# A diffusion transformer layer on one core: forward retention states made beside the last projection chunk, and retention and output tiles paced at 36 attention slots

## The chip, the core and the metric

The kernel runs on one core of a Trainium2 chip. The metric is the device time of one execution in microseconds. The core has a matmul engine (TensorE, PE in the profile; PEld is its weight load), a vector engine (VectorE, DVE), a scalar engine (ScalarE, ACT), GpSimd (POOL) and SyncE (SP), which issues the transfers here. Each engine works through its own queue of instructions in order and waits on semaphores for the others.

## The reference

One layer takes 2048 latent rows and 256 context rows of width 1024. All arithmetic is float32.

```python
h  = rmsnorm(x, norm1_g) * (1 + sc1) + sh1           # sh, sc, g: c_act @ w_mod + b_mod
hc = rmsnorm(ctx, norm1_g) * (1 + csc1) + csh1
rq, rk, rv, rg, aq, ak, av = split(h @ w_in)         # 512 512 512 512 512 128 128
crk, crv, cak, cav = (the same columns of) hc @ w_in # the context needs no others
# retention, 4 heads of 128, chunks of 128 rows, both directions, started from the context's state
o_fwd[c] = (q_c k_c^T * decay) v_c + q_c S_c * q_dec
S_(c+1)  = S_c * c_dec + (k_c * k_dec)^T v_c
ret = groupnorm(o_fwd + flip(o_bwd)) * gn_g * silu(rg)
# attention, 8 query heads on 2 key heads of 64, keys: 256 context + 2048 latent rows
att = softmax(rmsnorm(q) rope . rmsnorm(k) rope / 8) v
x = x + g1 * (concat(ret, att) @ w_out)              # w_out 1024 x 1024
x = x + g2 * (relu(h2 @ w_ff1) ** 2 @ w_ff2)         # h2 = rmsnorm, modulate; width 4096
out = rmsnorm(x, final_norm_g)
```

## The kernel before, in words

The float32 products are made of float16 ones. A factor is split into a high and a low part (`hi`, `lo`), and three matmuls (high by high, low by high, high by low) add up in one PSUM bank. In the traces they stand as three neighbouring lines: 638 to 640 in the projection, 1420 to 1422 in the output, 1668 to 1670 in the up product and 1728 to 1730 in the down product. Turns (transposes) and the retention products stay float32, as 128x128 matmuls.

**Start and projection.** Rows come in 18 tiles of 128: 0 and 1 are context, 2 to 17 latent (`x_c`, `x_l`). Ahead of the plan, code written out in order makes the modulation (`mods`, four quarters of `w_mod`) and prepares the first tiles: `squares` (line 444, ACT), `root` (lines 80 and 81, POOL), `normal` (line 450, DVE), then for each half p of the columns `turn_h` (line 459, PE), `modulate` (line 464 on DVE, 465 on POOL), `high_h` (line 469, ACT) and `low_h` (line 473, DVE). `first.fetch`, `bound`, `split` load the first weight chunk (`w_in` in four pairs of blocks), take its absolute bounds (line 506) and split it (lines 535, 536). `halves_h(p, ms)` does the four steps of a half for several tiles. Then comes the plan: `at(q, step, fn)` puts a step at clock q, and a loop over q runs the steps in the order `dma, mm, turn, copy, work, mix, extra, store`. A row of the projection (one tile by one column chunk, 24 matmuls) takes two clocks. The column chunks go in the order RV, RK, AKV, AQ, RG, RQ, of 18, 18, 18, 16, 16 and 16 rows; `base[col]` is a chunk's first clock. The row's bank is evacuated by ACT (line 645, `xs`).

Beside the rows the plan has other work: rope on DVE and POOL (lines 671, 674, 686) and the turn of its result (line 691), the norms of AKV and AQ heads (`ys`, `kn`; lines 723, 736), the turn of keys (`turn_key`, line 741), maxima over rows of weights (`maxima`; turns at line 386, `macc` at line 381), the tables of decay (`decay_tables`, ACT exponentials and a logarithm, lines 947 to 975), and the first maxima of the attention. The last are products of queries and keys, 18 pieces for each of the first groups (lines 167 and 171, PE), each followed by a DVE maximum (line 180, `nm`). Before the attention starts, `least` (lines 186 to 198) turns these into an extra row of the query.

**Attention.** 32 groups (a query tile by a key head) of 18 key pieces each, one piece to a slot k. `on(k, phase, fn)` puts an event at slot k, and the phases of a slot run in the order of `PHASES`. Scores start at slot 22 and take two matmuls a slot (lines 204 and 205); ACT makes the exponential (line 210) and its float16 part (line 214), DVE and POOL the rest (lines 221, 223), and PE the product with the values (lines 237, 238). Events in the same slots do the retention: `retention(24)` first makes 17 forward and 2 backward states, two slots each (a load of `rk` and `rv`; `weigh`, line 1229, POOL; `product`, line 1235, four matmuls; `update`, line 1245, DVE; a store of the forward state). From `R0 = 66` on, every `RF = 35` slots, a tile is made from the last to the first: three products (lines 1268 to 1270), and 43 slots later its output tile (`output_tile`: turn at line 1405, output product at lines 1420 to 1422). The first FF half needs the output tiles as well: the row norm (lines 1434, 1441, 1154, 1155), the normal `xr` (line 1447, POOL) that takes the new x back from memory, its turn (line 1452) and modulation (lines 1457, 1462). `output_weights(44)` loads and scales `w_out` (lines 1372, 1377).

**FF.** `prelude(done)` puts the first steps of the feed-forward part at the slots behind the last score (`done` = 606): loads and sums of `w_ff1` (`sum_w1`, line 1597, POOL), products (`up_part`), `gate_first` (line 1626, POOL). The loop runs to the slot of the last output tile's end; behind it FF runs to the end by itself.

## Time and profile before

| what | us |
|---|---|
| runs | 2898.58, 2898.51, 2896.85; median 2898.51 |
| profiled execution, its own time | 2894.32 |
| its span | 2892.2 |
| PE busy in the span | 2728.7 (94%) |
| stage: to the first latent turn | 0 to 62.6 |
| projection chunks, RV to the last evacuation | to 624 |
| attention, first score to last score | 632 to 1577.5 |
| from there to the first down matmul | to 1633.2 |
| FF to the end | to 2892 |

The profile's numbers belong to one execution, whose own time is 2894.32, so its span of 2892.2 covers nearly all of it. A row of the timeline gives start and duration; the bracket behind it is how long the engine had been idle and what released it. Matmuls of 128x512 issue every 0.216 us one behind the other, and their shown durations overlap. A row of the windows gives the window, its length, the busy time of the engines with the count of their instructions, the granted clock of PE, the share of DMA and the GB/s.

### The profile page before, as it was taken

How to read it: one execution, taken by the hardware profiler on the slowest of the kernel's cores; microseconds unless marked ns; L12 is line 12 of the kernel's file. 1: busy time of each engine (PE TensorE's matmuls, PEld its weight loads, DVE VectorE, ACT ScalarE, POOL GpSimd, SP SyncE). 2: the span in 40 equal slices, each digit the busy share in tenths (PEclk: the TensorE clock that was granted, in tenths of full speed). 3: DMA queues.
4: the chain of work that ended last, by engine and by line, in shares of the span. 5: the costliest groups of instructions: out<-in, count | busy, mean ns of one | idle time of the engine just before them, and what ended most of it. 6: DMA issues, size and time to landing. Idle time of an engine off the chain costs nothing. (4 is left out here: it accounts for less than half of the span.)

```text
span 2892.2 us, 45242 instructions
## 1 busy us (share of the span) xinstructions
PE 2728.7 (94%) x17152; PEld 1459.3 (50%) x17152; DVE 2094.2 (72%) x3324; ACT 1428.9 (49%) x2418; POOL 1528.8 (53%) x1289
## 2 busy tenths in 40 slices
PE   5999999988899998899999899999999999999998
PEld 2545644446566665566666344444444444444443
DVE  4556687667878777787785577777777777777776
ACT  3533762336777777777777333333333333333332
POOL 2523782338757568885667566664443434444432
PEclk8999999999999999999999999999999999999999
DMA  6478758337212213332113722231114411111111
GB/s 220 153 232 290 237 157 259 108 105 241 60 48 66 84 58 101 119 116 67 50 61 124 266 81 77 82 116 58 59 49 152 164 59 59 55 51 47 52 44 59
DMA packets 251320, 324.26 MB, mean 112 GB/s; under 512 B 106775, under 2 KB 157975, under 8 KB 249310
## 3 DMA queue, kind: packets, MB, share of 16 engines
q1 hardware_dynamic: 251102, 321.37, 34.5%
q8 instruction: 135, 2.21, 0.3%
q14 instruction: 83, 0.68, 0.1%
HBM read 249.84 MB, written 71.46 MB: 111 GB/s over the span
## 5 line engine op out<-in xcount | busy, mean ns | idle before, releaser
L180 DVE TENSOR_REDUCE nm<-mp 128x1 f32<-128x512 f32 (+1 forms) x576 | 389.5, 683 | 153.4 <-PE mp L167 124.6
L221 POOL TENSOR_TENSOR plo<-p,phi 128x1024 f16<-128x1024 f32 x160 | 353.1, 2208 | 165.6 <-ACT phi L214 136.2
L210 ACT ACTIVATE p<-st 128x512 f32<-128x512 f32 x576 | 337.8, 597 | 175.6 <-PE st L205 113.0
L1728 PE MATMUL pd<-w2hi,uhi 128*128 128x512 f16 x1024 | 388.1, 379 | 13.6 <-DVE acc L1731 13.3
L1729 PE MATMUL pd<-w2lo,uhi 128*128 128x512 f16 x1024 | 388.1, 379 | 0.6 <-DVE w2lo L72 0.6
L1730 PE MATMUL pd<-w2hi,ulo 128*128 128x512 f16 x1024 | 388.1, 379 | 0.0
L1731 DVE SCALAR_TENSOR_TENSOR acc<-pd,sc,acc 128x512 f32<-128x512 f32 x512 | 366.0, 738 | 5.7 <-PE pd L1730 5.6
L1668 PE MATMUL pu<-hf,w1f 128*128 128x512 f16 x896 | 340.3, 380 | 2.9 <-DVE q L1691 2.2
L1669 PE MATMUL pu<-hf,w1f 128*128 128x512 f16 x896 | 340.4, 380 | 0.0
L1670 PE MATMUL pu<-hf,w1f 128*128 128x512 f16 x896 | 340.2, 380 | 0.0
L214 ACT ACTIVATE phi<-p 128x1024 f16<-128x1024 f32 x288 | 303.9, 1055 | 0.0
L638 PE MATMUL pso<-whi,h 128*128 128x512 f16 (+1 forms) x816 | 294.9, 361 | 0.4 <-ACT whi L535 0.4
L639 PE MATMUL pso<-wlo,h 128*128 128x512 f16 (+1 forms) x816 | 294.5, 361 | 0.2 <-DVE wlo L536 0.2
L640 PE MATMUL pso<-whi,h 128*128 128x512 f16 (+1 forms) x816 | 294.5, 361 | 0.0
L237 PE MATMUL o<-wv,plo 128*128 128x65 f16 x2304 | 235.4, 193 | 22.9 <-POOL plo L221 16.8
L223 DVE TENSOR_TENSOR plo<-p,phi 128x512 f16<-128x512 f32 x256 | 236.1, 923 | 18.9 <-ACT phi L214 16.2
L238 PE MATMUL o<-wv,phi 128*128 128x129 f16 x2304 | 243.2, 221 | 0.0
L237 PEld LDWEIGHTS <-plo 128*128 128x128 f16 x2304 | 206.7, 98 | 57.3 <-POOL plo L221 25.6
L204 PE MATMUL st<-qr,ks 128*128 128x512 f16 x576 | 220.5, 383 | 15.1 <-ACT p L210 14.9
L1680 POOL TENSOR_TENSOR r<-r 128x512 f32<-128x512 f32 x64 | 66.3, 1039 | 295.2 <-ACT r L1679 295.2
L205 PE MATMUL st<-qr,ks 128*128 128x512 f16 x576 | 220.7, 383 | 1.1 <-DVE qr L198 1.0
L238 PEld LDWEIGHTS <-phi 128*128 128x128 f16 x2304 | 205.8, 98 | 20.0 <-issue 0.3
(326 smaller groups left out, 5393.9 us busy)
## 6 DMA issues: line engine op xcount, KB each, us to landing
wm<-in_w_ff SPq DMA_DIRECT2D x64, 512.0 KB, 5.2
w1r<-in_w_ff SPq DMA_DIRECT2D x64, 512.0 KB, 4.3
ws<-in_w_ff SPq DMA_DIRECT2D x124, 256.0 KB, 3.3
wmr<-in_w_mod SPq DMA_DIRECT2D x32, 512.0 KB, 5.5
hf<-hp SPq DMA_DIRECT2D x56, 256.0 KB, 3.2
hf<-hf SPq DMA_DIRECT2D x14, 1024.0 KB, 6.1
wst<-in_w_in SPq DMA_DIRECT2D x20, 512.0 KB, 6.1
orv<-rv SPq DMA_DIRECT2D x35, 256.0 KB, 3.0
```

What stands on the lines that cost most here:

```text
L180: nc.vector.tensor_reduce(dst, src, axis=AX.X, op=ALU.max, negate=True)
L210: nc.scalar.activation(self.p[kt // 2][:, kt % 2], self.s.pop(kt), AF.Exp, scale=HD**-0.5)
L221: nc.gpsimd.tensor_tensor(lo, p, hi, op=ALU.subtract)
L237: mm(o[:, : HD + 1], lo[:, i, c], v[:, : HD + 1], start=False, stop=False)
L238: mm(o, hi[:, i, c], v[:, :VW], start=False, stop=last)
L1668: mm(pu[i], whi, hi, start=k == 0, stop=False)
L1669: mm(pu[i], whi, lo, start=False, stop=False)
L1670: mm(pu[i], wlo, hi, start=False, stop=k == 3)
L1728: mm(ps, uh, wh, start=f == 0, stop=False)
L1729: mm(ps, uh, wl, start=False, stop=False)
L1730: mm(ps, ul, wh, start=False, stop=f == NF - 1)
L1731: nc.vector.scalar_tensor_tensor(acc[:, c], ps, sc2, acc[:, c], op0=ALU.mult, op1=ALU.add)
```

## The change

It has three parts. At the start the loads change places (all of the first weights ahead of x tiles 2 and 3), tile 2 goes from the written order into the plan, and the steps of tiles 0 and 1 stand among the splits in another order. In the plan, ten of the rows of maxima go into RV; the decay tables go from RQ to AKV and are cut in parts; the turns of keys and of queries come a clock later, and AQ goes from its last row to its first; the parts of the values go to RG; the first maxima of groups 0 and 1 are made in RG and those of group 2 in RQ; and the 17 forward states are made in RQ (15 of them, and two at the end) from the stores of RK and RV, every 29/16 clocks. In the attention only two backward states are left ahead of the tiles; tiles start at slot 34 every 36 slots; `output_weights` starts at slot 26; and the loop runs to the last event of all. The last output tile starts at slot 617 instead of 634.

```diff
@@ -278,7 +278,8 @@
             base[col] = 2 * len(slots)
-            slots += [(n, m) for m, t in enumerate(TILES) if t[0] == "l" or col not in (C_RQ, C_RG, C_AQ)]
+            ms = [m for m, t in enumerate(TILES) if t[0] == "l" or col not in (C_RQ, C_RG, C_AQ)]
+            slots += [(n, m) for m in (ms[::-1] if col == C_AQ else ms)]
@@ -472,10 +473,11 @@
-        for m in range(3, len(TILES)):
-            q = 2 * (m - 3)
+        for m in range(2, len(TILES)):
+            q = 2 * (m - 2)
...
                 at(max(0, q - 6), "dma", load_x, m)
+            if m > 2:
@@ -610,9 +612,9 @@
                     at(q + 2, "work", self.head_norm, 8)
-                    at(q + 3, "turn", self.turn)
-                    at(q + 4, "copy", self.split_turned)
-                    at(q + 5, "store", self.store_turned, aq_d)
+                    at(q + 4, "turn", self.turn)
+                    at(q + 5, "copy", self.split_turned)
+                    at(q + 6, "store", self.store_turned, aq_d)
@@ -625,8 +627,8 @@
                     at(q + 5, "copy", self.high_key)
-                    at(q + 6, "turn", self.turn_key)
-                    at(q + 7, "work", self.keep_key)
+                    at(q + 7, "turn", self.turn_key)
+                    at(q + 8, "work", self.keep_key)
@@ -939,28 +941,31 @@
-            def rates():
+            def rates(part):
...
...
             at(q0, "dma", load)
-            at(q0 + 3, "extra", rates)
-            for h in range(4):
-                at(q0 + 5 + h, "extra", tables, h)
-            at(q0 + 9, "extra", rest)
+            for i in range(4):
+                at(q0 + 6 + 2 * i, "extra", rates, i)
+                at(q0 + 14 + 3 * i, "extra", tables, i)
+            at(q0 + 26, "extra", rest)
+        def forward_states(c, q):
+            x = {}
+            def load():
+                x["k"] = sg.tile([P, 2, 512], F32, name="rkv", tag="wm")
+                for i, src in enumerate((rk_d, rv_d)):
+                    nc.sync.dma_start(x["k"][:, i], src[c])
+            def weigh():
+                x["w"] = sg.tile([P, 4, P], F32, name="rkw", tag="wmr")
+                k = x["k"][:, 0].rearrange("p (h d) -> p h d", h=4)
+                nc.gpsimd.tensor_tensor(x["w"], k, bc(kd[:, 0].unsqueeze(2), [P, 4, P]), op=ALU.mult)
+            def product():
+                x["ps"] = psM.tile([P, 4, P], F32, name="mpr", tag="mps", bufs=1)
+                for h in range(4):
+                    v = x["k"][:, 1, h * P : (h + 1) * P]
+                    mm(x["ps"][:, h], x["w"][:, h], v, start=True, stop=True)
+            def update():
+                old = states.get("s")
+                s = states["s"] = sg.tile([P, 4, P], F32, name="rst", tag="wst", bufs=4)
+                if old is None:
+                    nc.scalar.activation(s, x["ps"], AF.Copy)
+                    return
+                for h in range(4):
+                    nc.vector.scalar_tensor_tensor(
+                        s[:, h], old[:, h], cd[:, 0, h : h + 1], x["ps"][:, h], op0=ALU.mult, op1=ALU.add
+                    )
+            def store():
+                nc.sync.dma_start(sf_d[c - 1].rearrange("p (h d) -> p h d", h=4), states["s"])
+            at(q - 5, "dma", load)
+            at(q - 2, "mix", weigh)
+            at(q, "turn", product)
+            at(q + 1, "work", update)
+            if c > 0:
+                at(q + 1, "store", store)
...
             at(q_load, "dma", g.minima, kp)
+            assert len(qs) == NK
...
         rk, akv, aq, rg, rq = (base[c] for c in (C_RK, C_AKV, C_AQ, C_RG, C_RQ))
-        row_slots = [rk + 2 * i + 1 for i in range(18)] + [rg + 2 * i + 1 for i in range(14)]
+        row_slots = [11 + 2 * i for i in range(10)] + [rk + 2 * i + 1 for i in range(18)]
+        row_slots += [rg + 2 * i + 1 for i in range(4)]
@@ -1006,12 +1054,15 @@
             maxima(n, q)
-        value_parts(aq + 4)
-        decay_tables(rq)
-        ff_scales(rq + 13)
-        first_maxima(0, xp, "x", 4, rg + 8, [rg + 13 + i for i in range(18)])
-        first_maxima(1, sg, "wst", 4, rq, [rq + 4 + i * 12 // 17 for i in range(18)])
-        first_maxima(2, sg, "wst", 4, rq + 10, [rq + 17 + i * 12 // 17 for i in range(18)])
+        decay_tables(akv)
+        value_parts(rg + 2)
+        ff_scales(rq + 5)
+        states, end = {}, base["end"]
+        for c in range(NK - 1):
+            forward_states(c, rq + 4 + c * 29 // 16)
+        first_maxima(0, hp, "h0", 1, aq + 20, [rg + i * 16 // 18 for i in range(NK)])
+        first_maxima(1, hp, "h1", 1, aq + 24, [rg + 16 + i * 16 // 18 for i in range(NK)])
+        first_maxima(2, hp, "h0", 1, rg + 20, [rq + 2 + 2 * i for i in range(14)] + [end, end, end + 1, end + 1])
@@ -1027,8 +1078,8 @@
         loads = [[lambda q=q, k=k: mods[q].load(k) for k in range(0, KT, 2)] for q in range(4)]
-        between = [[lambda: load_x(0), lambda: load_x(1)], [lambda: load_x(2), lambda: first.fetch(0)]]
-        between += [[lambda k=k: first.fetch(k) for k in (2, 4, 6)], [lambda: load_x(3)]]
+        between = [[lambda: load_x(0), lambda: load_x(1)], [lambda k=k: first.fetch(k) for k in (0, 2)]]
+        between += [[lambda k=k: first.fetch(k) for k in (4, 6)], [lambda: load_x(2), lambda: load_x(3)]]
@@ -1047,12 +1098,9 @@
-        def halves_h(p, ms):
-            for m in ms:
-                turn_h(m, p)
-                modulate(m, p)
-                high_h(m, p)
-                low_h(m, p)
+        def first_half(m):
+            for fn in (turn_h, modulate, high_h, low_h):
+                fn(m, 0)
@@ -1060,26 +1108,28 @@
         mods[1].shift_and_scale()
-        modulation(2, (ready, 2), (halves_h, 0, (0,)), (first.bound, 0), (halves_h, 0, (1,)))
+        modulation(2, (first_half, 0), (first.bound, 0), (first_half, 1), (first.bound, 2))
...
         mods[2].shift_and_scale()
-        modulation(3, (halves_h, 0, (2,)), (first.bound, 2), (first.bound, 4), (first.bound, 6))
+        modulation(3, (first.bound, 4), (first.bound, 6))
...
         first.greatest()
+        modulate(0, 1)
         first.spread()
-        modulate(0, 1)
+        turn_h(1, 1)
         first.scales()
+        first.split(0)
...
         low_h(0, 1)
-        first.split(0)
         first.split(2)
-        halves_h(1, (1,))
+        modulate(1, 1)
         first.split(4)
+        high_h(1, 1)
+        low_h(1, 1)
         first.split(6)
-        halves_h(1, (2,))
-        ready(3)
+        ready(2)
@@ -1094,10 +1144,10 @@
+    pp = pool(attn, "pp", 3)
+    op = pool(attn, "op2", 2)
     qp = pool(attn, "qp")
-    op = pool(attn, "op2", 2)
     vp = pool(attn, "vp")
-    pp = pool(attn, "pp", 3)
@@ -1199,14 +1249,14 @@
     rp = pool(room, "rp", side="right")
-    BUFS = {"orv": 3, "ork": 2, "okw": 2, "oo": 2, "sf": 2, "sb": 2, "ma": 2}
+    BUFS = {"orv": 3, "ork": 2, "okw": 2, "oo": 2, "sb": 2, "ma": 2}
...
-    RF, R0 = 35, 66
+    RF, R0 = 36, 34
@@ -1246,9 +1296,6 @@
-        def keep_state(i):
-            nc.sync.dma_start(sf_d[i], x["s", i].rearrange("p h d -> p (h d)"))
@@ -1301,23 +1348,15 @@
-        SF = 2
-        todo = [(0, c) for c in range(NK - 1)] + [(1, 1), (1, 0)]
-        for n, (d, c) in enumerate(todo):
-            k = k0 + SF * n
+        for n, c in enumerate((1, 0)):
+            k = k0 + 2 * n
             on(k - 5, "dma", take, c, "rk", "rv")
-            on(k - 2, "late", weigh, d, c)
-            on(k, "pe", product, c, n % 2, (0, 1))
-            on(k + 1, "pe", product, c, n % 2, (2, 3))
-            if d == 0:
-                old, to, tag = None if c == 0 else ("s", c - 2), ("s", c - 1), "sf"
-            else:
-                old, to, tag = None if c == 1 else ("b", NT), ("b", NT - 1 + c), "sb"
-            on(k + 1, "late", update, d, c, old, to, tag, (0, 1))
-            on(k + 2, "late", update, d, c, old, to, tag, (2, 3))
-            if d == 0 and c > 0:
-                on(k + 3, "dma", keep_state, c - 1)
-        assert k0 + SF * len(todo) + 2 <= R0
+            on(k - 2, "late", weigh, 1, c)
+            on(k, "pe", product, c, n, (0, 1))
+            on(k + 1, "pe", product, c, n, (2, 3))
+            old = None if c == 1 else ("b", NT)
+            on(k + 1, "late", update, 1, c, old, ("b", NT - 1 + c), "sb", (0, 1))
+            on(k + 2, "late", update, 1, c, old, ("b", NT - 1 + c), "sb", (2, 3))
@@ -1489,7 +1528,7 @@
         for q in range(2):
-            at = k + (31 if t == 1 else 27) + q
+            at = k + (32 if t == 1 else 27) + q
@@ -1537,8 +1576,8 @@
     done = attention()
-    retention(24)
-    output_weights(44)
+    retention(25)
+    output_weights(26)
@@ -1786,7 +1825,7 @@
     with tc.manual_schedule():
-        for k in range(min(events)[0], max(made_at + 1, last) + 1):
+        for k in range(min(events)[0], max(events)[0] + 1):
```

Line numbers behind the first edit shift by 1 or 2, and those behind `decay_tables` by 39 to 50: 1420 to 1422 become 1459 to 1461, 1447 becomes 1486, 1597 becomes 1636, 1668 to 1670 become 1707 to 1709, and 1728 becomes 1767. The steps of a forward state are lines 1001 (load), 1006 (weigh), 1012 (product), 1018 and 1021 (update) and 1026 (store).

On ACT, at the start, ahead of the first square of a tile that the plan's first turn needs, there stood (`h` is the high half of a modulated tile, `ws` the bounds and `whi` the split of the first weights):

```order
L469 ACTIVATE h_535<-t 128x512
L506 ACTIVATE junk,ws<-wst 128x512 x6
L469 ACTIVATE h_479<-t 128x512
L535 ACTIVATE whi<-wst,ws 128x512 x4
L469 ACTIVATE h_502<-t 128x512
L535 ACTIVATE whi<-wst,ws 128x512 x4
L469 ACTIVATE h_535<-t 128x512
```

and now there stands:

```order
L470 ACTIVATE h_490<-t 128x512
L508 ACTIVATE junk,ws<-wst 128x512 x6
L537 ACTIVATE whi<-wst,ws 128x512 x2
L470 ACTIVATE h_467<-t 128x512
L537 ACTIVATE whi<-wst,ws 128x512 x4
L470 ACTIVATE h_490<-t 128x512
L537 ACTIVATE whi<-wst,ws 128x512 x2
L445 ACTIVATE junk,ss<-x_l_371 128x1024
```

The third tile's halves are gone from this place, and the splits stand in pairs between the halves of the first two.

On DVE, at the end of RQ, the last rows of the projection (`t` and `ys` are the rope, `unit` and `mt` open the attention) read before:

```order
L671 TENSOR_TENSOR t_6481<-xs,tb_6388 128x512
L180 TENSOR_REDUCE nm<-mp 128x2
L686 TENSOR_TENSOR ys<-t_6481,t_6482 128x512
L671 TENSOR_TENSOR t_6511<-xs,tb_6439 128x512
L686 TENSOR_TENSOR ys<-t_6511,t_6512 128x512
L1112 TENSOR_TENSOR unit<-ident 128x1
```

and now, with `rst` for the forward states:

```order
L673 TENSOR_TENSOR t_6753<-xs,tb_6661 128x512
L1021 SCALAR_TENSOR_TENSOR rst<-rst,cd,mpr 128x128 x4
L688 TENSOR_TENSOR ys<-t_6753,t_6754 128x512
L180 TENSOR_REDUCE nm<-mp 128x1 x2
L1021 SCALAR_TENSOR_TENSOR rst<-rst,cd,mpr 128x128 x4
L180 TENSOR_REDUCE nm<-mp 128x1
L180 TENSOR_REDUCE nm<-mp 128x2
L1162 TENSOR_TENSOR unit<-ident 128x1
```

Two states' updates and four maxima stand behind the last row's first rope step.

On POOL, in the tail behind the last score, the normal of the last output tile (`xr`) stood behind the sums of the up weights (`w1s`) and the gated down weights (`w2r`):

```order
L1597 TENSOR_TENSOR w1s<-w1r 128x512
L1462 TENSOR_TENSOR u<-u,s_240 128x512 x2
L1597 TENSOR_TENSOR w1s<-w1s,w1r 128x512
L1626 TENSOR_TENSOR w2r<-w2r,g2h 128x512 x2
L1597 TENSOR_TENSOR w1s<-w1r 128x512
L1626 TENSOR_TENSOR w2r<-w2r,g2h 128x512
L1680 TENSOR_TENSOR r<-r 128x512
L1626 TENSOR_TENSOR w2r<-w2r,g2h 128x512
L1597 TENSOR_TENSOR w1s<-w1r,w1s 128x512
L1154 TENSOR_SCALAR cv_f<-ss 128x1
L1155 TENSOR_TENSOR cy_f<-cv_f,half 128x1
L1447 TENSOR_SCALAR xr<-xr,cy_f 128x1024
```

and now stands ahead of them:

```order
L1204 TENSOR_SCALAR cv_f<-ss 128x1
L1205 TENSOR_TENSOR cy_f<-cv_f,half 128x1
L1486 TENSOR_SCALAR xr<-xr,cy_f 128x1024
L1636 TENSOR_TENSOR w1s<-w1r 128x512
L1636 TENSOR_TENSOR w1s<-w1s,w1r 128x512
L1665 TENSOR_TENSOR w2r<-w2r,g2h 128x512 x2
L1636 TENSOR_TENSOR w1s<-w1r 128x512
```

`xr` of the last tile has moved up past four of the sums and four of the gated weights.

37 lines of the change are left out of this document (20 added, 17 removed).

## The prediction

> **What bounds the kernel now.** I read the page's busy shares first, then the windows of the stages, then the waits, chain and timeline inside the stages that the diff touches. TensorE bounds the whole.
>
> ```profile
> PE 2728.7 (94%) x17152; PEld 1459.3 (50%) x17152; DVE 2094.2 (72%) x3324; ACT 1428.9 (49%) x2418; POOL 1528.8 (53%) x1289
> ```
>
> 94% is a mean over stages, so the stages are laid side by side. The rows are the first 48.7 us, the projection chunks AKV, AQ and RQ, the tail behind the last score, and FF.
>
> ```profile
> 0.00:48.70 48.70, 27.57 (x162) 10.55 (x163) 16.95 (x70) 13.64 (x30) 8.19 (x18) 0.87 0.85 285
> 276.40:334.20 57.80, 52.92 (x473) 46.06 (x472) 31.24 (x105) 45.04 (x108) 33.08 (x78) 1.00 0.79 247
> 334.20:427.10 92.90, 90.41 (x452) 45.20 (x450) 72.34 (x123) 59.08 (x112) 75.97 (x84) 1.00 0.60 185
> 523.50:625.00 101.50, 98.27 (x485) 48.38 (x483) 66.19 (x157) 28.14 (x52) 30.45 (x36) 1.00 0.27 83
> 1578.00:1633.00 55.00, 47.35 (x265) 23.80 (x264) 25.88 (x43) 19.87 (x39) 31.09 (x32) 0.97 0.84 317
> 1633.00:2892.00 1259.00, 1229.78 (x5682) 555.56 (x5680) 932.77 (x1213) 426.00 (x686) 567.24 (x432) 1.00 0.24 78
> ```
>
> The first two numbers are length and busy PE. The projection is nearly full (RQ 98.3 of 101.5), so an instruction put into PE's order there costs its issue time. FF, the last row, is the same code in the same order: 0. What can be won is idle PE at the start, waits inside the chunks, slots of attention that are long for another engine's sake, and the tail.
>
> **A, the start.** This is the longest gap of PE in the kernel.
>
> ```profile
> 53.29 0.63 ACT L469 ACTIVATE h<-t 128x512 f16<-128x512 f32 x1 [2.75 <-POOL t L465]
> 59.12 0.63 ACT L469 ACTIVATE h<-t 128x512 f16<-128x512 f32 x1 [2.75 <-POOL t L465]
> 62.63 1.09 PE L459 MATMUL psx<-ident,x_l 128*128 128x128 f32 x4 [10.51 <-DVE x_l L450]
> DMA  0598899999999999999997250385000000002898
> ```
>
> ACT waits twice for POOL (2.75 each), once for the half of tile 1 and once for that of tile 2, ahead of the square (line 444) that releases the next tile. In the new order tile 1's modulation stands on DVE ahead of split 4, so that the first wait has splits under it, and tile 2 has left this chain (second wait, and its 0.63). That is 2.75 + 2.75 + 0.63 = 6.1: **−6**. All of it lies on the path, since PE waits for the end of this chain alone. x tiles 2 and 3 are now issued on SP's queue behind all pairs of w_in halves, but the same transfers stand ahead of the last of them. The last row above is the DMA share over 0 to 75 us, 1.9 us a digit: these loads are over by 53, so a later tile 2 is still in time for a square at 54 or so. Bounds: 0, where it lands late by as much as ACT gains, and −10.5, the whole gap; I take the value that the two waits show.
>
> **B, the projection.** The change adds 15 forward states (a POOL product, four fp32 matmuls, four DVE updates, a load and a store each) to RQ. Ten rows of maxima (a turn on PE and DVE work each) go from RG to RV, pieces of the first maxima from RQ to RG, the decay tables from RQ to AKV. Prices on PE:
>
> ```profile
> 663.94 0.61 PE L1235 MATMUL bank<-orv,okw 128*128 128x128 f32 x4
> 664.38 0.38 PE L204 MATMUL st<-qr,ks 128*128 128x512 f16 x1
> 1592.76 0.38 PE L1421 MATMUL bank<-wo,ah 128*128 128x512 f16 x1
> 1592.98 0.38 PE L1422 MATMUL bank<-wo,al 128*128 128x512 f16 x1
> ```
>
> Four fp32 products issue in 0.44 (663.94 to 664.38), one 128x512 matmul in 0.22 (start to start; the shown 0.38 overlaps). The waits, and the pieces in RQ:
>
> ```profile
> PE psx L741 <- DVE kn L736: 4.5, 5, 1.4
> PE psx L691 <- DVE ys L723: 4.0, 4, 1.7
> PE mps L386 <- DVE macc L381: 1.7, 2, 0.9
> PE mp L167 <- DVE nm L180: 1.8, 4, 1.0
> L180 DVE TENSOR_REDUCE nm<-mp 128x1 f32<-128x512 f32 (+1 forms) x36 | 23.8, 683 | 0.5 <-PE mp L167 0.4
> ```
>
> - RV: ten rows of a 0.44 turn would be 4.4; PE's idle behind the start gap takes most of it, and I take +1.4 (bounds 0 and 4.4).
> - AKV: turn_key one step later removes most of 4.5 (−4.3); the decay tables move onto ACT there.
>
> ```profile
> 528.90 0.69 ACT L645 ACTIVATE xs<-pso,wm 128x512 f32<-128x512 f32 x1 [4.43 <-PE pso L640]
> 529.61 1.28 ACT L947 ACT_TABLE_LOAD   x1
> 530.90 0.21 ACT L947 ACTIVATE dw<-dw 128x8 f32<-128x8 f32 x1
> 531.13 1.28 ACT L949 ACT_TABLE_LOAD   x1
> 537.72 1.28 ACT L972 ACT_TABLE_LOAD   x1
> ```
>
>  Three loads (3.9) and 4.7 of small exponentials are 8.6 us more on ACT, which is busy 45.0 of 57.8 there. The cover is its 12.8 of idle time, but the tables fall on the chunk's first two thirds, and ACT's evacuations free PE's banks behind them: I take +3.0 as not covered (bounds 0 and 8.6). Sum −1.3. Silu and Exp each need one reload more, two times 1.28, of which the first stands ahead of an evacuation in RG that has slack of 4.4 (the first row above) and the second ahead of the first attention exponential.
> - AQ: turn one step later, −4.0, the whole row of waits.
> - RG: 36 pieces where 18 were, 18 × 0.22 = +3.9, less the 1.7 of waits for macc, as ten rows have left: +2.2.
> - RQ: of the 36 pieces (x36) 14 stay. 15 × 0.44 = +6.6, 22 × 0.22 = −4.8, waits for nm −1.0, and +2 for products that find rk and rv not landed: +2.8. Their loads (17 of 512 KB) stand in SP's queue among the stores, in a window with a DMA share of 0.27, so they should rarely be late; who waits behind a late product is the row of projection matmuls on PE, hence ACT's evacuation. Bounds 0 and 15 (1 us a product). POOL and DVE cover the rest: 15 products of 1.2 (below) on a POOL busy 30.5 of 101.5, 60 updates of 0.34 against 22 maxima of 0.68 less, on a DVE busy 66.
> - Handover: DVE has eight updates (0.34 each, in C) and four maxima (0.68) more behind the last evacuation:
>
> ```profile
> 624.07 0.69 ACT L645 ACTIVATE xs<-pso,wm 128x512 f32<-128x512 f32 x1 [2.27 <-PE pso L640]
> 633.68 0.58 PE L205 MATMUL st<-qr,ks 128*128 128x512 f16 x1 [0.99 <-DVE qr L198]
> ```
>
>  From evacuation to first score product 633.68 − 624.07 = 9.6 now, with PE waiting for DVE. Of the 5.4 us of DVE that come in, I let its waits for ACT and POOL there take 3.1: +2.3 (bounds 0 and +5.4).
>
> Sum of B: 1.4 − 1.3 − 4.0 + 2.2 + 2.8 + 2.3 = **+3.4**.
>
> A rule weighed against these rows: the Trainium skill, "ScalarE: Activation LUTs", section "What ACT_TABLE_LOAD costs", puts a switch at about 1.28 us of load plus 1.38 us of drain. By it the three loads in AKV would take 8.0, not 3.9, and the sum would come out some 4 us higher. The trace agrees on the load and not on the drain: 528.90 + 0.69 is 529.59, the load starts at 529.61 and the exponential at 530.90.
>
> **C, attention, slots 22 to 597.** Line 204 issues once a slot, so windows cut at its count give slot lengths: 12 slots (46 to 57), 180, 120 and 168.
>
> ```profile
> 666.80:694.00 27.20, 5.01 (x13) 1.29 (x13) 0.87 0.94 306
> 773.30:1065.60 292.30, 68.16 (x180) 17.54 (x181) 1.00 0.20 63
> 1065.60:1269.80 204.20, 45.90 (x121) 11.71 (x120) 0.98 0.34 99
> 1269.80:1545.00 275.20, 63.64 (x169) 16.36 (x168) 1.00 0.23 72
> ```
>
> Slots 46 to 57 take 27.2, where 12 at the later 1.62 take 19.5; the DMA share is 0.94 there. Between 658 and 694:
>
> ```profile
> ACT wo L1377 <- POOL wos L1372: 8.7, 2, 7.1
> PE bank L1235 <- POOL okw L1229: 5.3, 5, 3.2
> L1245 DVE SCALAR_TENSOR_TENSOR sf<-sf,cd,bank 128x128 f32<-128x128 f32 x36 | 10.5, 341 | 15.7 <-DMA sf<-sf 12.9 <-PE bank L1235 2.8
> L1229 POOL TENSOR_TENSOR okw<-ork,kd 128x512 f32<-128x512 f32 x10 | 11.7, 1170 | 5.0 <-DMA ork<-rk 5.0
> ```
>
> All but the wait for wos belong to forward states, which leave; output weights come earlier, onto emptier slots. So 27.2 goes to about 19.2: **−8**, the last retention states and the first tile (slot 34) taking the place of the rest at the rate of a later slot. On PE the stage is even: 17 states out (17 × 0.44 = 7.5), the last output tile in. Bounds: −15.5, where those 7.5 are time as well, and +10, if the output tile's work (10 us of PE, in D) lands on slots with no room.
>
> **D, the tail.** From the last score to the first down matmul:
>
> ```profile
> 1577.46 0.38 PE L205 MATMUL st<-qr,ks 128*128 128x512 f16 x1
> 1604.39 0.66 PE L1452 MATMUL bank<-ident,xr 128*128 128x128 f32 x4 [1.77 <-POOL xr L1447]
> 1627.25 1.12 POOL L1447 TENSOR_SCALAR xr<-xr,cy_f 128x1024 f32<-128x1024 f32 x1 [5.11 <-DMA x<-xr]
> 1628.42 0.66 PE L1452 MATMUL bank<-ident,xr 128*128 128x128 f32 x4 [3.89 <-POOL xr L1447]
> 1633.19 0.38 PE L1728 MATMUL pd<-w2hi,uhi 128*128 128x512 f16 x1
> ```
>
> 1633.19 − 1577.46 = 55.7. The last output tile now starts at slot 617 rather than 634. Behind the last score the program's order has 60 output matmuls instead of 96: 36 × 0.22 = 7.8, with 2 of products and turns that go along, about 10. Of the waits 3.89 goes and 1.4 of the 1.77, because the last tile's normal (xr) comes before the up matmuls run out: 5.3. That makes −15.3. What is late next: POOL's xr waits for a store of x to land (5.11), and in the new order it stands ahead of w1 sums for the up matmuls, so these queue behind the wait, and PE behind them. I give back 4 of the 5.1: **−11** (bounds −18, with the second wait gone and nothing given back, and 0).
>
> Sum: −6 + 3.4 − 8 − 11 = −21.6 against the profiled execution's 2894.3, so 2872.7. The median of the runs, 2898.5, stands 4.2 above; the forecast in its terms is **2877**.
>
> **Rivals.**
> - More than that (0.15): no late product, no give-back on POOL: −6 + 0 − 10 − 15 = −31, so 2867. For it: POOL is busy only 31 of 55 in the tail, and RQ's DMA is at 0.27. Against it: xr has waited for x in the last tiles already, whoever was behind it.
> - The tail's gain is lost (0.18): D = 0, since the first down matmul waits for POOL's w2 products behind the store, whenever PE is done with the tile; 2888. For it: the 5.11, and a DMA share of 0.84 in that window. Against it: the up matmuls, 28 rows of work, stand between.
> - No measurable change (0.14): the 15 products wait for rk and rv on PE, at 1.1 us each +16.5 in place of +2 (the row for sf has 12.9 in 6, 2.2 a time): −21.6 + 14.5 = −7, and with a start held by its loads −1: 2892 to 2898.
> - Slower (0.08), by one mechanism: at 36 slots per tile every tile begins at the same phase of the 18-slot group (at 35 the phase moves by one a tile). If that phase is the crowded one, all 576 slots run like slots 286 to 405: 204.2/120 = 1.70 against 292.3/180 = 1.62 and 275.2/168 = 1.64. 576 × 0.06 = +35 or so: 2877 + 35 = 2912. It decides from 1.69 a slot on (27 us). Against it: 16 tiles passed through 16 phases before, and both long windows are level.
>
> **How the numbers follow.** The forecast has 0.45, with its own range 2868 to 2889. All four parts at their better end give −10.5 + 0 − 15.5 − 15 = −41, 2858, the low end; the high end is the no-change case's, 2898, above which the slower case (0.08) lies. 0.2% is 5.8 us, about what can be told from no change. Faster: 0.45 + 0.15 + 0.18, and 0.01 of the no-change case, which begins just below 2892.7: 0.79; the same 0.13; slower 0.08.
>
> **What would show it.** PE's first gap ends near 56 instead of 62.6 (A). AKV and AQ lose their waits for kn and ys; RQ's length stays within 2 us of 101.5, with no PE wait for rkv (B). Slots 46 to 57 take about 19 (C). Last score to first down takes about 45, and POOL has xr before w1s (D). The prediction is wrong if the slot rate passes 1.68, if RQ grows by over 10 us, or if the tail keeps 55.

## The result: slower by 1.4%, and the profile after

| | before | changed |
|---|---|---|
| runs, median | 2897.68 (2892.78 to 2898.58) | 2938.52 (2936.88 to 2939.62) |
| span of the profiled execution | 2892.2 | 2937.8 |

The ratio is 1.0144, with a 95% interval of 1.0130 to 1.0158. Forecast were 2877 and a range of 2858 to 2898, so the forecast missed in sign. Each of the three things that the prediction named as showing it wrong came true: a slot rate over 1.68 (1.702 over slots 124 to 555), RQ over 10 us longer (11.0), and a tail that keeps its 55 (54.7).

The lengths of the stages, from the start of a stage's first matmul to that of the next, come from the two traces:

| stage | before | changed | difference | the prediction's term |
|---|---|---|---|---|
| to the first projection matmul | 48.8 | 45.2 | −3.6 | A: −6, with the first gap, which lies in RV |
| RV | 123.3 | 126.5 | +3.2 | +1.4 |
| RK | 104.4 | 104.9 | +0.5 | 0 |
| AKV | 57.7 | 64.0 | +6.3 | −1.3 |
| AQ | 93.0 | 89.6 | −3.4 | −4.0 |
| RG | 96.4 | 100.5 | +4.1 | +2.2 |
| RQ, to its last matmul | 99.8 | 110.8 | +11.0 | +2.8 |
| handover to the first score | 8.7 | 9.6 | +0.9 | +2.3 |
| first to last score | 945.2 | 961.7 | +16.5 | C: −8 |
| last score to first down matmul | 55.9 | 54.7 | −1.2 | D: −11 |
| FF from there | 1259.0 | 1270.1 | +11.1 | 0 |

The windows of the changed kernel that answer to those of before are these: the time to the first matmul, AKV, AQ, RQ, the tail and FF.

```profile
0.00:45.20 45.20, 25.80 (x154) 8.39 (x155) 14.27 (x66) 11.34 (x26) 6.42 (x15) 0.92 0.93 307
276.60:340.60 64.00, 55.66 (x473) 47.11 (x472) 38.20 (x138) 51.53 (x127) 33.57 (x80) 0.97 0.72 228
340.60:430.30 89.70, 89.70 (x449) 44.99 (x447) 66.33 (x111) 58.40 (x109) 72.19 (x87) 1.00 0.61 184
530.80:641.60 110.80, 107.48 (x576) 59.83 (x574) 64.45 (x157) 19.64 (x31) 47.87 (x48) 0.98 0.52 172
1613.00:1667.70 54.70, 39.92 (x216) 19.62 (x215) 18.96 (x25) 15.03 (x28) 28.27 (x26) 0.89 0.82 317
1667.70:2937.00 1269.30, 1234.77 (x5680) 556.59 (x5679) 944.96 (x1223) 429.36 (x692) 570.53 (x435) 0.99 0.24 76
```

AQ is full (89.7 busy of 89.7): there the change did what it says. RQ is full too, and longer: it carries more PE work than the prediction counted. AKV is longer with PE idle for 8.3 of 64. The tail has PE idle for 15 of 54.7. FF has the code of before, and its 10.3 us more than in the row of before are 5.3 of idle PE and 5.0 of busy PE (1234.77 against 1229.78, for as many matmuls). The granted clock of the row is 0.99 instead of 1.00.

The start, in the timeline, with the first gap and the two places in RV where PE waits for DVE:

```profile
55.40 1.12 PE L460 MATMUL psx<-ident,x_l 128*128 128x128 f32 x4 [4.52 <-DVE x_l L451]
...
114.43 0.63 PE L460 MATMUL psx<-ident,x_l 128*128 128x128 f32 x4 [1.82 <-DVE x_l L451]
115.78 1.46 PE L387 MATMUL mps<-macc,ones 128*32 128x512 f32 x2 [0.73 <-DVE macc L382]
```

The first gap fell from 10.51 to 4.52, by the 6.0 that were forecast; RV gave it back, in part here.

A forward state in RQ, in PE's timeline, and the count of its products over the whole run:

```profile
561.53 1.05 PE L1012 MATMUL mpr<-rkv,rkw 128*128 128x128 f32 x8
562.42 0.38 PE L640 MATMUL pso<-whi,h 128*128 128x512 f16 x1
...
L1012 PE MATMUL mpr<-rkv,rkw x136: 272/275/348, 544.4 to 645.5; 128*128 128x128 f32 x136
```

Four heads are eight records (136 for 17 states) and 562.42 − 561.53 = 0.89 of issue, not 0.44.

The tail, in the timelines of POOL and PE:

```profile
1656.89 1.12 POOL L1486 TENSOR_SCALAR xr<-xr,cy_f 128x1024 f32<-128x1024 f32 x1 [8.54 <-DMA x<-xr]
1657.98 1.26 POOL L1636 TENSOR_TENSOR w1s<-w1r 128x512 f32<-128x512 f32 x1
1659.32 1.26 POOL L1636 TENSOR_TENSOR w1s<-w1s,w1r 128x512 f32<-128x512 f32 x1
1660.54 2.48 POOL L1665 TENSOR_TENSOR w2r<-w2r,g2h 128x512 f32<-128x512 f32 x2
...
1667.70 0.59 PE L1767 MATMUL pd<-w2hi,uhi 128*128 128x512 f16 x1 [6.16 <-ACT w2hi L71]
1674.46 0.59 PE L1767 MATMUL pd<-w2hi,uhi 128*128 128x512 f16 x1 [3.49 <-ACT w2hi L71]
```

POOL stands 8.54 for the store of the last x tile; the sums and the gated down weights stand behind it, ACT's split behind these, and PE waits for that split at its first down matmuls. These take 0.59 each, where the first one before took 0.38. PE has half its clock for 12 us there, as this row of the windows shows (0.50):

```profile
1667.70:1679.60 11.90, 5.90 (x14) 2.05 (x14) 9.88 (x12) 5.52 (x10) 5.41 (x5) 0.50 0.00 0
```

Its 14 matmuls keep PE busy for 5.9, about 3 more than 14 × 0.22.

In the attention the mean slot from 124 to 555 is 1.702 instead of 1.643 us. Averaged over the tiles by the offset from a tile's first slot (36 offsets, from the starts of line 204), two slots stand out: offset 4 with 4.18 and offset 34 with 4.40, where the others take 0.65 to 2.66. Offset 34 of the eighth tile, where it took 5.6, in the timelines of POOL, ACT and PE:

```profile
1145.83 1.09 POOL L255 TENSOR_TENSOR ma<-so 128x256 f32<-128x256 f32 x1
1146.99 0.61 POOL L256 TENSOR_TENSOR ma<-ma,r 128x256 f32<-128x256 f32 x1
1147.56 1.27 POOL L1300 TENSOR_TENSOR oqf<-oqt,tf 128x512 f32<-128x512 f32 x1
1148.82 1.12 POOL L1486 TENSOR_SCALAR xr<-xr,cy_f 128x1024 f32<-128x1024 f32 x1
1149.90 2.55 POOL L221 TENSOR_TENSOR plo<-p,phi 128x1024 f16<-128x1024 f32 x1
1149.99 0.66 PE L1491 MATMUL bank<-ident,xr 128*128 128x128 f32 x4 [1.59 <-POOL xr L1486]
1152.48 0.60 ACT L210 ACTIVATE p<-st 128x512 f32<-128x512 f32 x1 [3.46 <-POOL plo L221]
```

POOL has the group's combine (lines 255, 256), a decay (1300) and the normal (1486) in a row, 4.1 us in all, ahead of the low part of the exponential (221), and ACT waits 3.46 for the buffer that this frees. Offset 4 of the same tile, 30 slots earlier:

```profile
1095.33 2.12 POOL L221 TENSOR_TENSOR plo<-p,phi 128x1024 f16<-128x1024 f32 x1 [0.27 <-ACT phi L214]
1095.45 2.56 DVE L223 TENSOR_TENSOR plo<-p,phi 128x512 f16<-128x512 f32 x1
1097.93 0.68 DVE L180 TENSOR_REDUCE nm<-mp 128x1 f32<-128x512 f32 x1
1098.66 0.38 PE L167 MATMUL mp<-ks,qr 128*128 128x512 f16 x1 [2.16 <-DVE nm L180]
1100.60 0.63 PE L204 MATMUL st<-qr,ks 128*128 128x512 f16 x1
```

Here DVE has the low part, takes 2.56 for it and is late with the maximum, and PE waits 2.16. (The score at 1100.60 takes 0.63 instead of 0.38: behind this wait PE has half its clock for 3.4 us.) The 2.56 are what makes the slot long. In the changed kernel line 223 takes 0.66 to 0.8 in most places, but 2.5 at this one in twelve tiles, the third to the tenth and the twelfth to the fifteenth. Each time POOL's line 221 had begun 0.1 to 0.2 us before it, and line 223 ended 0.55 us behind the end of that instruction. In these tiles offset 4 takes 4.1 to 4.9. In the eleventh tile the two lines began together, POOL's took the longer time, and offset 4 took 2.1:

```profile
1291.61 2.69 POOL L221 TENSOR_TENSOR plo<-p,phi 128x1024 f16<-128x1024 f32 x1 [3.40 <-ACT phi L214]
1291.63 0.68 DVE L223 TENSOR_TENSOR plo<-p,phi 128x512 f16<-128x512 f32 x1
1292.96 0.38 PE L167 MATMUL mp<-ks,qr 128*128 128x512 f16 x1 [0.20 <-DVE nm L180]
```

From slot 80 or so to the end of the attention PE's waits for `nm` are 30.6 us, and 10.5 before.

### The profile page after: what moved, and what is told of

The parts are those of the page before. It is cut to its first block, busy times and chain, and to the rows that moved or that the text cites. A ratio compares the mean times of both kernels' runs of the same rounds, so it can differ in the third digit from the quotient of the medians.

```text
span 2937.8 us, 45247 instructions
## 1 busy us (share of the span) xinstructions
PE 2745.8 (93%) x17152; PEld 1467.0 (50%) x17152; DVE 2144.4 (73%) x3324; ACT 1428.8 (49%) x2419; POOL 1530.4 (52%) x1289
## 5 line engine op out<-in xcount | busy, mean ns | idle before, releaser
L640 PE MATMUL pso<-whi,h 128*128 128x512 f16 (+1 forms) x816 | 298.1, 365 | 1.3 <-ACT whi L537 1.3
L642 PE MATMUL pso<-whi,h 128*128 128x512 f16 (+1 forms) x816 | 297.5, 365 | 0.0
L223 DVE TENSOR_TENSOR plo<-p,phi 128x512 f16<-128x512 f32 x256 | 255.8, 1001 | 34.7 <-ACT phi L214 28.4
L167 PE MATMUL mp<-ks,qr 128*128 128x512 f16 x512 | 195.8, 383 | 38.0 <-DVE nm L180 37.8
```

## The experiments

Medians are given with the median of the kernel before that ran beside them; stage lengths come from each run's trace.

**The pace and the phase.** Tiles every 35 slots from slot 50:

```diff
-    RF, R0 = 36, 34
+    RF, R0 = 35, 50
```

> The changed kernel with tiles every 35 slots from slot 50 instead of every 36 from slot 34, so that the last output tile starts at the same slot (618 against 617) but the phase of the tiles in the 18-slot group moves by one a tile. Theory (the pace of 36 puts the same two events of each tile on the same crowded slots): the first to last score take 943 to 950 us instead of 961.7, the two slots of over 4 us a tile are gone, the median falls from 2938.5 to 2922-2928. Rival (it is the work packed ahead of the last score, whatever its phase): first to last score stays within 958 to 965, median 2935-2940.

Measured 2925.04 (before 2898.36, ratio 1.0077 to 1.0107), score stretch 945.5. So 16 us of what the attention lost are the pace of 36 from slot 34, with as much work packed ahead of the last score. The 945.5 are still 18.6 over the old timing of the tiles (926.9, below), and what part of these is the packed work was not separated. The same pace from slot 43 (`RF, R0 = 36, 43`):

> The changed kernel with the pace of 36 kept and the first tile at slot 43 instead of 34: every tile starts at phase 3 of the 18-slot group instead of 12, the last output tile at slot 626. Theory (phase): again a pattern that repeats every 36 slots, with its long slots at other offsets; the score stretch differs from 961.7 by 5 us or more. Rival (density alone): 958 to 963. The tail behind the last score gets some 6 us longer in both, as nine slots more of the last tile lie in it.

Measured 2909.83 (ratio 1.0024 to 1.0049), stretch 928.7, 33 less than from slot 34. A fixed phase is no loss as such: phase 3 is better than a drift, phase 12 worse. The windows from first to last score of the changed kernel, of the first run and of this one (line 204 alone):

```profile
651.30:1613.00 961.70, 222.18 (x576) 56.80 (x575) 0.98 0.25 77
```

```profile
654.20:1599.70 945.50, 221.13 (x576) 56.57 (x575) 0.99 0.26 78
```

```profile
652.90:1581.60 928.70, 220.07 (x576) 56.34 (x575) 0.99 0.26 79
```

Two more phases (`R0 = 46` and `R0 = 40`):

> The changed kernel with the first tile at slot 46 (phase 6 of the group; the last output tile at 629). Theory of the phase: the stretch of scores lies away from both 961.7 (phase 12) and the drift's 945, nearer to phase 3's 928.7, as the combine of the group then falls in none of the tile's crowded slots: 925 to 940. Rival (phase 3 is a lucky place): 945 to 965.

> The changed kernel with the first tile at slot 40 (phase 0 of the group; the last output tile at 623). With the pace of 35 the tiles that began at phases 2 to 0 took 1.72 to 1.80 us a slot in the kernel before, though two h pairs ran beside them. Theory of the phase: a stretch of its own between 930 and 955. Rival (the stretch depends on how early the tiles start, 34 the worst, 43 the best): 940, between 961.7 and 928.7 in proportion.

One execution each: 2895.95 with a stretch of 924.4, and 2900.2 with 924.9 (before 2896.07). Phases 0, 3 and 6 are alike, so neither an early start nor a lucky place explains it. (With other edits beside them, in runs below, the two starts gave 924.4 and 926.8 again.) The start at 46 alone brings the changed kernel from 2938.5 back to the time of before. It also has FF at 1258.0: there the last tile's normal again comes behind FF's first gates.

**Which work collides at phase 12.** The two decays on POOL earlier:

```diff
-            on(k - 10, "dma", take, c, "qt", "kt")
-            on(k - 5, "late", decay, c, "qf", tf)
+            on(k - 12, "dma", take, c, "qt", "kt")
+            on(k - 8, "late", decay, c, "qf", tf)
...
-            on(k - 3, "late", decay, c, "qb", tb)
+            on(k - 7, "late", decay, c, "qb", tb)
```

> The changed kernel (pace 36 from slot 34) with the two decays of the query (POOL, line 1300, 1.3 to 1.7 us each) three and four slots earlier, at 8 and 7 slots ahead of the tile instead of 5 and 3, and the query's load two slots earlier. Theory (at this phase POOL's combine of the group, the decays and the normal xr stand together ahead of the low part of the exponential at offset 34): the slot of 4.4 us at offset 34 falls to 2 to 3 us, the score stretch from 961.7 to 930-945, the slot of 4.2 at offset 4 stays; median 2908-2924. Rival (offset 34 is long because PE waits for xr itself): the long slot stays above 4 and the stretch above 955.

Measured 2929.64 (before 2896.07, ratio 1.0092 to 1.0130), stretch 950.6. The theory's slot was missed: offset 34 rose from 4.40 to 5.68, and offset 4, which was to stay, fell from 4.18 to 2.14. The moved decay stood in POOL's queue just ahead of the combine, and ACT's waits for POOL's `plo` doubled over the stretch (33.4 in the changed kernel), while those for DVE's went from 37.8 to nearly nothing:

```profile
ACT p L210 <- POOL plo L221: 66.1, 28, 4.0
ACT p L210 <- DVE plo L223: 0.4, 1, 0.4
```

No line 223 of over 2 us is left at offset 3 or 34, and offset 4 takes 2.14 in nearly every tile. So the two long slots have causes of their own: POOL's queue at offset 34, the meeting of the two low parts at offset 4. The normal two slots later, with its turns:

```diff
-        on(made + 4, "late", norm)
+        on(made + 6, "late", norm)
...
-            at = k + (32 if t == 1 else 27) + q
+            at = k + (32 if t == 1 else 29) + q
```

> The changed kernel (pace 36 from slot 34) with the normal of the output tile on POOL (xr) two slots later, and the turns of xr and what follows two slots later. Theory (at offset 34 POOL reaches the low part of the exponential late, because the combine of the group, a step of an h pair and the normal stand ahead of it, all of them of this phase): the slot of 4.4 us at offset 34 falls below 3, another slot rises by at most 1, and the score stretch falls from 961.7 by 10 to 25 us. Rival (the crowd only moves, as it did when the decays were moved): a long slot of 4 or more at another offset, stretch 955 to 965.

Measured 2911.64 (before 2894.80, ratio 1.0038 to 1.0065), stretch 935.9. The gain of 26 is what the theory's upper end gave, but not by its mechanism alone: offset 34 fell by 1.3 only (4.40 to 3.14, where below 3 was forecast), offset 4 fell by 2.3 (the meeting is gone there too), and offsets 0 and 1 rose by 1.0 and 1.6. ACT's waits for the low parts over the stretch, in the changed kernel and with the normal later:

```profile
ACT p L210 <- DVE plo L223: 37.8, 33, 1.7
ACT p L210 <- POOL plo L221: 33.4, 16, 3.5
```

```profile
ACT p L210 <- DVE plo L223: 14.3, 33, 0.9
ACT p L210 <- POOL plo L221: 13.2, 15, 1.5
```

Both fall, by 23.5 and 20 us, where the stretch falls by 26. The same edit at phase 6 (with the tables beside AQ, below):

> First tile at slot 46, decay tables beside AQ, and the normal and the turns of xr two slots later. At phase 6 the slot at offset 34 still takes 3.6 us. Theory (POOL's backlog is the cause there too): it falls to 2.5 or less, the score stretch from 924.4 by 8 to 16 us, the whole to 2876-2884. Rival (at this phase the move crowds another slot): 922 to 930, whole 2888-2894.

Measured 2918.46 (before 2897.10, ratio 1.0057 to 1.0083), stretch 948.4 instead of 924.4. The slot at offset 34 did fall as the theory says (3.63 to 1.63), but offsets 0 and 1 rose from 2.59 and 1.08 to 3.88 and 3.61. The rival holds, with a wait that names its cause, on PE over the stretch:

```profile
PE bank L1444 <- DVE u L1496: 23.1, 14, 1.9
```

The later turns of xr, at offsets 36 and 37, take the bank that the next tile's turn of the attention's result needs at 37 (11 and 6 slots ahead of 43 are its two turns). At phase 12 this wait came too (13.2), under a larger gain. The edit in the kernel before, where tiles drift (with the start and the later turns of keys and queries, which a run below has alone; the turns of xr stay where they were):

> The kernel before with the start and the later turns of the change (2890.2) and the normal two slots later, its turns where they were; tiles every 35 slots, so that each tile has another phase. Theory (POOL's backlog at the normal): the stretch of 945.7 falls by 3 to 10 us, as only some of the phases have it: 2880-2887. Rival (a drift hides nothing): 944 to 948, 2889-2892.

Measured 2914.76 (before 2897.10, ratio 1.0044 to 1.0071), stretch 972.4 instead of 945.7: a loss of 27 that neither side forecast. The turns of xr were left one slot behind the normal, and PE waits for it in 13 tiles:

```profile
PE bank L1452 <- POOL xr L1447: 25.6, 13, 3.3
```

Phase 8 (`R0 = 48`, tables beside AQ):

> As the one before with the first tile at slot 48 (phase 8). Theory (only some phases are crowded, and 12 is the worst seen; 0, 3 and 6 gave stretches of 924.4 to 928.7): 920 to 932, whole 2886-2894. Rival (the stretch goes up with the phase from 6 towards 12): 935 to 950, whole 2898-2912.

Measured 2910.58 (before 2894.80, ratio 1.0037 to 1.0068), stretch 940.0: the stretch rises from phase 6 (924.4) over 8 (940.0) to 12 (961.7), as the rival had it.

**The attention's old timing.** `RF, R0 = 35, 66` and `output_weights(44)` in the changed kernel, states still in RQ:

> The changed kernel with the attention's old timing (first tile at slot 66, every 35 slots, output weights from slot 44), while start, projection and forward states in RQ stay changed. Theory: first score at 651 as in the changed kernel, the score stretch 935 to 941 (before: 945.2, less the 8 us of the states), tail and FF as before (56 + 1259), so about 2903-2910. Rival (the attention is slower for another reason than its tiles' timing, such as the pools' order): the score stretch stays above 950, and the time above 2917.

Measured 2906.47 (before 2898.36, ratio 1.0017 to 1.0036), stretch 926.9, tail 62.6, FF 1258.6. Against the kernel before the stretch is 18.3 shorter, but the tail 6.7 longer: together 11.6 are won there, by the states' departure and the little else that changed in the attention, and RQ pays 10.2. The changed kernel's stretch is 34.8 longer than this one, so that is the price of the tiles' (and the output weights') new timing.

**The tail.** On POOL the sums and gates ahead of the last normal:

```diff
-                on(k0 + 27 + 2 * i + n, "late", gate_first, i, n)
+                on(k0 + 19 + 2 * i + n, "late", gate_first, i, n)
...
-            on(k0 + 24 + 2 * i, "late", sum_w1, 1, *SUMS1[i])
+            on(k0 + 18 + i, "late", sum_w1, 1, *SUMS1[i])
```

> The changed kernel with the sums of the second block of up weights and the gating of the first down weights issued 6 to 10 slots earlier, so that on POOL they stand ahead of the normal of the last output tile, which waits for the store of x. Theory (POOL's order makes PE's first down products late): PE's gaps of 6.2, 1.7 and 3.5 us around the first down matmul go, the time falls by 8 to 11 us to 2927-2930. Rival (the loads of the down weights are late themselves, as they are issued behind 7 MB of other loads): less than 3 us, 2935-2939.

Measured 2932.70 (before 2898.36, ratio 1.0102 to 1.0132): 5.8 less than the changed kernel, between the two. PE's waits for the split of w2 fell from 9.6 to 2.5, and a wait of 3.3 for xr is new:

```profile
PE bank L1491 <- POOL xr L1486: 3.3, 1, 3.3
PE pd L1767 <- ACT w2hi L71: 2.5, 2, 1.2
```

**The projection.** The rows as before (`row_slots` of the kernel before):

> The changed kernel with the steps of the later modulation rows where they were (none in RV, 14 in RG). Theory (the ten steps cost RV what the start gained): in RV the two sums on PE (lines 387, some 1.7 us each) and their waits of 2.2 and part of the 3 us of waits for x_l leave, so RV falls from 126.5 by 5 to 7 us; RG takes the same two sums and waits, +3 to +5 on 100.5, so the whole falls by 1 to 3 us only, to 2935-2938. Rival (RV is held by loads, not by these steps): RV stays within 2 us and the whole rises by 3 to 5, to 2942.

Measured 2937.75 (before 2898.14, ratio 1.0119 to 1.0149). RV fell from 126.5 to 121.8, RG rose from 100.5 to 108.1: the ten steps cost RV 4.7, and would cost RG more beside its 36 pieces. (The runs that leave RV alone have it at 126.5 to 129.6, so 4.7 is the least.) The tables beside AQ (`decay_tables(aq)`):

> The changed kernel with the decay tables made beside AQ instead of AKV. Theory (three table loads, the exponentials on ACT and the small DVE steps delay the keys' norm in AKV): AKV falls from 64.0 to 57-59 us, its waits for kn from 6.8 to 2 or less, and AQ, whose rows are twice as long, rises by 0 to 2 us from 89.6; whole 2932-2935. Rival (the turn of the keys one clock later is what costs AKV): AKV stays above 62.

Measured 2930.09 (ratio 1.0089 to 1.0119), AKV 57.3 and AQ 89.6: the tables cost AKV 6.7 and AQ nothing. PE's wait for the keys' norm in AKV, in the changed kernel and here:

```profile
PE psx L743 <- DVE kn L738: 6.8, 4, 2.8
```

```profile
PE psx L743 <- DVE kn L738: 1.9, 4, 1.0
```

Half of each state's products:

> The changed kernel with only two of the four heads' products in each forward state (the updates take the two twice, so states and output are those of other sums). Theory (a state costs 0.89 us of PE in RQ, twice the 0.44 that the prediction took): the 15 rows' time falls by 15 x 0.44 = 6.6, RQ from 110.8 to 103-105. Rival (RQ is longer because the loads of rk and rv arrive late on SP's queue): RQ keeps 108 or more. Nothing else moves by more than 2 us; whole 2930-2933.

Measured 2932.08 (ratio 1.0097 to 1.0142), RQ 105.3: 5.5 less for 15 × 0.44 = 6.6 of PE. RQ takes 108.5 to 112.9 in the runs that leave the states as they are, so the fall is outside their spread, and its size is known to some 2 us. RQ's excess is PE's issue time, mostly.

Start and turns alone, in the kernel before:

> The kernel before with two parts of the change alone: the start (load order, tile 2 in the plan, the order of the first steps) and the turns of keys and queries one clock later (AQ's rows in their old order). Theory: the first gap on PE falls by 6 us, one more turn in RV takes 0.9 back, AKV and AQ lose 4 us of waits each, so 2884-2890. Rival (the start's gain is lost in RV to loads and later x tiles, and the later turn of the keys moves their wait elsewhere): 2892-2898, as before within 0.2%.

Measured 2890.18 (before 2898.14, ratio 0.9957 to 0.9979), just above the theory's span. To the end of RV it is 5.3 ahead of before (45.6 + 121.2 against 48.8 + 123.3), AKV is 0.9 shorter (56.8) and AQ 3.3 (89.7). The key's later turn is worth less than the 4.3 of the prediction.

**Together.** First tile at 43, tables beside AQ and the gates:

> The changed kernel with the first tile at slot 43, the decay tables in AQ, and on POOL the sums and gates of FF's first weights ahead of the last tile's normal. If the three gains add up (2938.5 - 28.7 - 8.4 - 5.8): 2895.6, 2892-2899, as the kernel before within its uncertainty. If the sums and gates are no gain where the tail is longer (slot 626): 2900-2904.

First tile at 46 and the tables:

> The changed kernel with the first tile at slot 46 and the decay tables beside AQ. Sum of the two single edits: 2895.95 - 8.4 = 2887.5; 2885-2891, faster than the kernel before by 0.2 to 0.4%. Rival (the first tile at 46 was measured by one run, which may have been a low one): 2892-2897, no difference from before.

First tile at 40, tables, normal and gates:

> First tile at slot 40 with all three edits (tables beside AQ, normal two slots later, FF's first sums and gates ahead of the last tile's normal on POOL). The sum of the single gains on 2900.2: -8.4 for the tables, -5.8 for the gates, -5 to -15 for the normal: 2871-2881. If the normal's move crowds another slot at phase 0: 2884-2890.

Measured 2898.63 (before 2896.07, ratio 0.9998 to 1.0017), 2891.48 (before 2894.80, 0.9974 to 0.9992) and 2890.30 (before 2897.10, 0.9970 to 0.9988). The second and third are faster than the kernel before, and beat the changed one by 47 and 48 us. The third has a stretch of 926.8 where 924.9 stood without the normal's move: no gain from it at phase 0, so its sum was 9 to 19 us too good. None is better than start and turns alone.

## Why the prediction was wrong

The stages together came out 67 us above their terms: C 24.5, the tail with FF 20.9, RQ 8.2, AKV 7.6, the start with RV 4.2, and less in the rest.

- **C, the phase, is the step that failed most, and in sign.** The states' departure was under-rated (−8 forecast, −18.3 measured in the stretch with the old timing); the 17 states that were put at 7.5 of PE in its bounds are 17 × 0.89 = 15.1, by the misreading that RQ has below. But the pace was priced at nothing in the forecast and given 0.08 as a rival, at 35 us. The rival's mechanism is what happened, in its size too (961.7 is 37 more than at phases 6 and 0): it decided from 1.69 a slot on, and slots 124 to 555 took 1.702. Its evidence against was a mean over tiles at all phases, which cannot tell one phase from the next. By tile, the starts of line 204 before give from 1.54 to 1.80 a slot. That spread was the warning, though the tile at phase 12 took 1.54 there: with 35 slots a tile meets its neighbour elsewhere, so the phase's price could not be read from a drift. What collides is of two kinds. At offset 34 the normal of one tile, the group's combine and the next tile's decays queue on POOL; but that slot is long at the good phase 6 too (3.60 against 4.40). At offset 4 DVE's low part meets POOL's. Phase 12 is 3.47 us a tile longer than phase 6, of which offset 4 has 2.28 and offset 34 has 0.80. The runs show that moving the normal takes 26 us off at phase 12; no run moves line 223 alone, so the share of offset 4 rests on the traces.
- **D** failed in sign too, if FF is counted with it: the give-back was named, with its cause, and set at 4, and with FF's 11.1 it was larger than the gain. The store of x, 5.11 of waiting before, took 8.54, and the w2 split came late after the first down matmul as well, where the term looked no further: FF's 0 was +11.1, about half of it idle PE and half busy PE, most of the latter in the 12 us at half the clock. With the order on POOL mended 5.8 come back; starts at 46 and 48, with the last tile later, have FF at 1258.
- **RQ**: the price of a state was half of what it is, as four records of two heads were read as four heads: 15 × 0.89 = 13.3 in place of 6.6. With it the term is 9.5, and 11.0 were measured. The 2 us for late loads have 3.3 beside them (gaps of 2.51 and 0.81 ahead of line 1012), for which the profile names no releaser.
- **AKV**: the tables cost 6.7, inside the bounds of 0 to 8.6, where 3.0 was taken; the later key turn brought 0.9, not 4.3. By the Trainium skill, "ScalarE: Activation LUTs", "What ACT_TABLE_LOAD costs", a drain of about 1.38 us comes on top of the load at every switch to a different set of tables. The trace of the changed kernel shows the load (1.28) and no drain, as ACT's timeline in AKV has it:

```profile
304.15 0.19 ACT L820 ACTIVATION_READ_ACCUMULATOR junk<-wm 128x1 f32 x1
304.36 1.28 ACT L977 ACT_TABLE_LOAD   x1
305.65 0.31 ACT L977 ACTIVATE dT<-dw 128x128 f32<-128x128 f32 x1
```

  The 6.7 hold the loads and all the small steps of the tables; no run here separates them.
- **A and RV**: the gap shrank by 6.0, as worked out. RV's term was mis-sized because the ten steps were taken for rows of maxima with a 0.44 turn. They are sums of modulation rows: two DVE multiply-adds a step, and every fourth a float32 product over 512 columns (line 387). They cost RV 4.7 rather than 1.4.
- **AQ and the handover** came out within 1.4 of their terms, RG within 2.

## What to carry to other kernels

Ahead of a change of a pace, lay the period of the new work over the period of the old: a drift averages over the collisions, a common period picks one and pays it every time, for good or ill, and the first slot decides which. Work taken out of a stage in which PE has slack and put into one that PE fills is paid at full price there, so count its records in the trace, head by head. Ahead of a wait that moves up in an in-order queue, look at everything that stands behind it, also past the point at which the stage seems to end.

## What was not expected of the hardware

A float32 128x128 product over data is two records of 0.11 us on PE, a turn by the identity one (L1012 x8 in 0.89 for four heads, L693 x4 in 0.44 for four blocks, 558.29 to 558.73).

DVE's line 223 and POOL's line 221 don't overlap freely. Begun 0.12 us behind POOL's at 1095.33, DVE's took 2.56 and ended 0.56 behind it; begun within 0.02 us of it at 1291.61, DVE's took 0.68, and POOL's 2.69 instead of 2.12. Of the 256 of line 223 in the changed kernel 23 took over 2 us, all of them behind the start of a running line 221 (in 12 tiles at offset 3, in 10 at offset 34). So an order of a tenth of a microsecond between two engines that don't wait for each other cost PE about 2 us a tile (offset 4 with 4.1 and more against 2.1). No run here separates what the two lines share.
